# Scores on half the rows, rotary halves exchanged by transfers, two units' values copied at once, another order of block sums: one decoder block on one core

## The chip, the cores and the metric

The kernel runs on one core of one Trainium2 chip. The metric is the device time of one execution in microseconds. A core has TensorE (PE in the profile; its loads of weights are PEld), VectorE (DVE), ScalarE (ACT), GpSimd (POOL) and SyncE (SP), each with a queue of its own that it works off in order. SP issues the transfers (DMA) of this kernel. Matrix products land in PSUM, which has eight banks of 128 x 512 f32; everything else is in SBUF.

## What is computed

One decoder block over 512 tokens of width 1024: a SwiGLU feed-forward layer, a token-mixing layer, a second SwiGLU layer, each behind an RMS norm with shift, scale and gate from a conditioning vector, and a final RMS norm. The change lies in the mixing layer and, in one place, at the start of the second feed-forward layer. Cut to what matters:

```python
def apply_rope(t, cos, sin):
    t1, t2 = jnp.split(t, 2, axis=-1)
    return jnp.concatenate([t1 * cos - t2 * sin, t2 * cos + t1 * sin], axis=-1)

# token_mixing: proj = u @ w_in, split into p, q, k, v, gate_logits
q = apply_rope(q.reshape(B, S, N_ATTN_HEADS, HEAD_DIM), cos, sin)   # 12 heads of 64
k = apply_rope(k.reshape(B, S, N_ATTN_HEADS, HEAD_DIM), cos, sin)
for gi, (window, dilation) in enumerate(((128, 1), (512, 4), (2048, 16))):
    # 4 heads each: query t attends to keys t - j*dilation, j = 0..window // dilation
    o, lse = dilated_window_attention(...)
# groups are combined by the softmax of their log denominators
merged = g_pool * (y_pool @ w_pool_branch) + g_attn * (y_attn @ w_attn_branch)
return merged @ w_out
```

## The kernel before

Products with weights keep f32 accuracy by three terms: each weight chunk is split into a high half (`whi`, an ACT copy at L298) and a low half (`wlo`, a DVE subtraction at L310), each activation likewise (`UH`, `UL`), and a product is high x high, high x low and low x high (`mm3`, L341 to L343). Weights come from HBM as chunks of 512 KB into three buffers `raw` (`fetch`, L226); `look` keeps the splits up to three chunks ahead of use, and a chunk is loaded as soon as a buffer is free and the program has reached that call. SP's queue holds these loads in program order.

The order of everything is written out by hand: each engine does its instructions in the order in which the Python emits them. `mm_tile` (L990) is one tile of 128 output features by 512 tokens: 8 k-steps of three 128x512 products; at chosen k-steps it calls hooks, which emit the attention's instructions in between.

The mixing layer runs as follows. `head` makes the first four tiles, q and k of group 0, in four banks `bk`. Before the change each tile held the first or the second 32 features of four heads (`qk_cols`), so that both rotary halves of all heads lay in two banks, row by row. `rope` (L974) made four products with cosine and sine of both banks (L981) and then, for each pair of heads (64 rows), the difference and the sum (L987, L988) into `qt` or `kt`; there a head pair `hp` has 512 columns, and a head's 64 features lie in rows that are spread as two times 32. For groups 1 and 2 the sums also reorder the tokens into four classes, a stride of four elements on the read. Then v of group 0 is made (L1222 to L1225), then eight tiles for q and k of groups 1 and 2, two pool tiles (`pool_diff`, on GpSimd), four class tiles for v of groups 1 and 2 (L1272 to L1278), and the gates.

Attention is worked in units `(kind, n, hp)`: kind 0 is group 0 with a block n of 128 queries, kind 1 is groups 1 and 2 together with a class n of 128 tokens, hp one of two pairs of heads. A unit passes through four steps, spread over three tiles by `hooks` (L1232):

- `at_prep` (L1010): q times a mask that leaves one head's rows (`qz`, L1018), so that a product over all 128 rows gives one head's scores.
- `at_scores` (L1022): the score products (L1035 and L1037 for kind 0, L1041 for kind 1) into the half `h` of one of two banks `bS`, which take turns by unit; then mask and row maximum (L1053), the negated maximum (L1055) and the exponential with its sum (L1058).
- `at_turn` (L1062), a tile later: transposes of the probabilities (L1070) and a copy (L1073 or L1076).
- `at_values` (L1079), another tile later: products with v (L1093) into `bO`, and a copy of it (L1095, for kind 0 after every unit; L1097, for kind 1 after both).

For kind 0 each of eight tiles takes one new unit; for kind 1 each of four tiles takes two.

The second feed-forward layer works pairs of tiles by block sums of activations. `u_steps` (L673) gives the sums (DVE, L679 and L695) and the splits of three of them into high and low halves `S` (ACT at L685, DVE at L686); `ffn2` (L787) emits them as a list `todo` between the first tiles.

Of the kernel before, what the change touches and what calls it, by code (L numbers as in the profile page):

```python
# [8 lines left out]
F32 = mybir.dt.float32  # L9
# [5 lines left out]
P = 128  # L15
# [74 lines left out]

# [46 lines left out]
class Kernel:  # L137
# [535 lines left out]
    def u_steps(self, n):  # L673
# [7 lines left out]
        def split(i, u):  # L681
            def f():
                hi, lo = self.S[i]
                if i < 3:
                    nc.scalar.activation(hi, u, AF.Copy)  # L685
                    v.tensor_tensor(lo, u, hi, op=OP.subtract)  # L686
                    return
                nc.scalar.activation(hi, u.rearrange("p (k t) -> p k t", k=4), AF.Copy)
                v.tensor_tensor(lo, u.rearrange("p (k t) -> p k t", k=4), hi, op=OP.subtract)
            return f  # L690

# [95 lines left out]
    def ffn2(self):  # L787
        self.put, self.now = [], 0
        bk = [self.nb() for _ in range(4)]
        self.head(2, bk, AF.Silu)  # L790
        adds, (s2, s1, s0, last) = self.u_steps(2)
        self.todo = adds[:3] + [s0, adds[3], s2, adds[4], s1, adds[5]]
        do = lambda n: [self.todo.pop(0)() for _ in range(n)]
        for j in range(2):
            self.ffn_post(j, self.ffn_silu(j, bk[2 * j]), bk[2 * j + 1])
            do(2 + j)
# [4 lines left out]
        self.ffn(2, 4, last)  # L801

# [170 lines left out]

    def rope(self, pa, pb, dst, classes=1):  # L974

        v = self.nc.vector
        t = [self.rt.tile([P, 528], F32, name=f"rt{i}")[:, :T] for i in range(4)]
        for o, x, y in ((t[0], pa, self.cos), (t[1], pb, self.sin), (t[2], pb, self.cos), (t[3], pa, self.sin)):  # L980
            v.tensor_tensor(o, x, y, op=OP.mult)  # L981
        for half in (0, 1):
            rows = slice(64 * half, 64 * half + 64)
            cols = slice(T * half, T * half + T)
            src = [x[rows].rearrange("p (i c) -> p c i", c=classes) for x in t]
            to = [dst[r, cols].rearrange("p (c i) -> p c i", c=classes) for r in (slice(0, 64), slice(64, 128))]
            v.tensor_tensor(to[0], src[0], src[1], op=OP.subtract)  # L987
            v.tensor_tensor(to[1], src[2], src[3], op=OP.add)  # L988

# [19 lines left out]

    def at_prep(self, u):  # L1010

        kind, n, hp = u
        gs, toks = self.at_tokens(u)
        qz = self.aw.tile([P, T], F32, name="qz")
        for i, g in enumerate(gs):
            q = self.qt[g][:, hp * T:hp * T + T]
            for h in range(2):
                self.nc.vector.tensor_scalar(qz[:, (2 * i + h) * P:(2 * i + h + 1) * P], q[:, toks],  # L1018
                                             self.hmask[:, h:h + 1], None, op0=OP.mult)
        self.qz[u] = qz  # L1020

    def at_scores(self, u):  # L1022
        kind, n, hp = u
        nc = self.nc
        M = nc.tensor.matmul
        self.si ^= 1
        S = self.bS[self.si]
        qz = self.qz.pop(u)
        gs, toks = self.at_tokens(u)
        for h in range(2):  # L1030
            o = h * 256
            if kind == 0:
                k = self.kt[0][:, hp * T:hp * T + T]
                if n == 0:
                    M(S[:, o + P:o + 2 * P], qz[:, h * P:h * P + P], k[:, 0:P], start=True, stop=True)  # L1035
                else:
                    M(S[:, o:o + 2 * P], qz[:, h * P:h * P + P], k[:, (n - 1) * P:(n + 1) * P], start=True, stop=True)  # L1037
            else:
                for i, g in enumerate(gs):
                    k = self.kt[g][:, hp * T:hp * T + T]  # L1040
                    M(S[:, o + i * P:o + i * P + P], qz[:, (2 * i + h) * P:(2 * i + h + 1) * P], k[:, toks],  # L1041
                      start=True, stop=True)
        p = self.aw.tile([P, T], F32, name="prob")
# [7 lines left out]
        for h in range(2):  # L1051
            cs = slice(h * 256 + c0, h * 256 + 256)
            nc.vector.tensor_tensor_reduce(p[:, cs], S[:, cs], mask[:, c0:], 1.0, 3.0 * NEG, op0=OP.add, op1=OP.max,  # L1053
                                           accum_out=mx[:, h:h + 1])
# [24 lines left out]
    def at_values(self, u):  # L1079
# [4 lines left out]
        for h in range(2):  # L1084
# [7 lines left out]
            for i, (blk, v) in enumerate(srcs):  # L1092
                M(o, pt[:, blk * P:blk * P + P], v, start=i == 0, stop=i == len(srcs) - 1)  # L1093
        if kind == 0:
# [78 lines left out]
    def mix(self):  # L1173
        nc, tc = self.nc, self.tc
        v, M = nc.vector, nc.tensor.matmul
        self.prob, self.probT, self.pd, self.qz = {}, {}, {}, {}
        self.si = self.ti = 0
        outer = ExitStack()
# [3 lines left out]
        with tc.tile_pool(name="ma", bufs=1) as ma, tc.tile_pool(name="rt", bufs=1) as self.rt, \  # L1182
# [29 lines left out]
            for n in range(4):  # L1212
                if n:
                    self.split(self.pos + n - 1)
                    self.fetch()
                if n == 3:
                    self.at_prep((0, 0, 0))
# [13 lines left out]

            def hooks(new, extra=(), nxt=()):  # L1232
                h = {}
# [3 lines left out]
                for i, u in enumerate(sc):  # L1237
                    h.setdefault(3 + i, []).append(lambda u=u: self.at_turn(u))
                for i, u in enumerate(new):
                    if u not in self.qz:  # L1240
                        h.setdefault(i, []).insert(0, lambda u=u: self.at_prep(u))
                    h.setdefault(5 + i, []).append(lambda u=u: self.at_scores(u))
                for u in nxt:
                    h.setdefault(6 + len(new) - 1, []).append(lambda u=u: self.at_prep(u))
                for k, f in extra:
# [13 lines left out]
            b = self.mm_tile(hooks([], nxt=g23[0]))  # L1259
            self.pool_diff(0, b)  # L1260
            b = self.mm_tile(hooks(g23[0], nxt=g23[1]))
            self.pool_diff(1, b)
# [85 lines left out]
    def build(self):  # L1348
# [23 lines left out]
        self.ones = tl("ones", P)  # L1372
        self.invf, self.hmask, self.icnt, self.ident = cst[:, 0:1], cst[:, 1:3], cst[:, 3:35], cst[:, 35:163]
        self.cst = cst
# [143 lines left out]
def constants():  # L1518
    i = np.arange(P)
    invf = (ROPE_THETA ** (-np.arange(0, HEAD_DIM, 2) / HEAD_DIM)).astype(np.float32)  # L1520
    hm = np.stack([(i % 64 // 32 == h) for h in range(2)], axis=1).astype(np.float32)
    cnt = np.zeros((P, 32), np.float32)
    for t in range(2):
        for half in range(2):
# [4 lines left out]
    q, k = i[:, None], i[None, :]  # L1529
    return np.concatenate([invf[i % 32][:, None], hm, cnt, np.eye(P, dtype=np.float32),  # L1530
                           neg(k >= q), neg(k <= q), neg((k <= q) & ((q - k) % 4 == 0))], axis=1)
# [42 lines left out]
```

## Time and profile before

Three runs took 1013.68, 1013.88 and 1016.19 us; the median is 1013.88.

| what | us |
|---|---|
| the profiled execution's own time | 1014.89 |
| its span, first to last instruction | 1013.1 |
| granted clock of TensorE, mean | 0.999 |
| DVE, v1 to the last class tile (378 to 516), low halves L310 | 23.0 |
| the same, masks L1018 | 15.3 |
| the same, rotary products L981 | 15.3 |
| the same, rotary sums L987 and L988 | 4 x 5.7 |
| ACT busy, 378 to 535 | 54.7 |
| DVE busy, 378 to 535 | 105.5 |
| TensorE busy, 378 to 535 | 156.7 |

The profile is of one execution. A busy time is the union of an engine's instructions. TensorE's matmuls overlap, one starting before the last has run out, and their ends are modelled; so for TensorE the distance between starts tells its pace better than the length of a record. An f32 matmul leaves two records of load and product, the split products of `mm3` one each. The chain of waits is followed back from the last instruction, and its pieces do not overlap.

### The profile page before, as it was taken

The page shows a single profiled execution, that of the slowest core. Times are in us where ns is not written, and L with a number is a line of the kernel's source. Part 1 is how long each engine was busy: PE and PEld are TensorE (multiplying, and loading weights), DVE is VectorE, ACT ScalarE, POOL GpSimd, SP SyncE. Part 2 cuts the span into 40 slices and gives each one's busy share as a digit, 9 for nine tenths or more (in the row PEclk, how much of TensorE's full clock was granted, in tenths as well). Part 3 has the DMA queues.
Part 4 walks back from the last instruction along what each step waited for, and adds up shares of the span by engine and source line. Part 5 has one row for each costly group of instructions (what it writes and reads, how often), then busy time and mean ns, then how long its engine had stood idle before and what let it go on. Part 6 is the DMA issues. An engine that isn't in the chain of part 4 may idle for free.

```text
span 1013.1 us, 15788 instructions
## 1 busy us (share of the span) xinstructions
PE 1004.4 (99%) x6460; PEld 912.8 (90%) x6460; DVE 763.9 (75%) x1117; ACT 442.8 (44%) x674; POOL 26.9 (3%) x31
## 2 busy tenths in 40 slices
PE   9999999999999999999999999999999999999997
PEld 7888999989899999889988888998899899998997
DVE  7989979789797677878447776577787776676754
ACT  6443644525435443334424323454365255352553
POOL 0000000000000000008000000000000000000002
PEclk9999999999999999999999999999999999999999
DMA  9755456455454323122155773412344234241312
GB/s 338 274 202 209 146 160 221 149 173 169 152 182 136 104 77 104 61 65 84 32 199 177 257 270 107 125 56 69 88 167 125 81 105 146 84 137 51 100 47 83
DMA packets 43146, 139.61 MB, mean 138 GB/s; under 512 B 4929, under 2 KB 8257, under 8 KB 43074
## 3 DMA queue, kind: packets, MB, share of 16 engines
q1 hardware_dynamic: 42498, 138.08, 41.4%
q8 instruction: 50, 0.82, 0.3%
q10 hardware_dynamic: 576, 0.52, 0.2%
q14 instruction: 22, 0.18, 0.0%
HBM read 135.82 MB, written 2.77 MB: 137 GB/s over the span
## 4 chain that ended last, share of the span: by engine, by line
PE 87%; DVE 7%; issue 2%; DMA 2%; ACT 1%; POOL 0%; SPq 0%; POOLq 0%; DVEq 0%; ACTq 0%
PE bank L342 15%; PE bank L343 15%; PE bank L341 15%; PE bank L719 10%; PE bank L721 10%; PE bank L720 10%; DVE wlo L310 2%; PE bank L1501 1%; PE bank L1503 1%; PE bank L1505 1%; PE bank L1093 1%; PE bank L1272 1%; DVE H L864 1%; PE bank L1273 1%; PE bank L1274 1%
## 5 line engine op out<-in xcount | busy, mean ns | idle before, releaser
L310 DVE TENSOR_TENSOR wlo<-raw,whi 128x1024 fp32r<-128x1024 f32 (+6 forms) x166 | 174.3, 1061 | 66.0 <-ACT whi L298 65.7
L298 ACT ACTIVATE whi<-raw 128x1024 fp32r<-128x1024 f32 (+6 forms) x166 | 149.9, 920 | 49.2 <-DVE raw L242 41.5
L719 PE MATMUL bank<-UH,whi 128*128 128x256 f32 x544 | 150.6, 277 | 0.2 <-ACT u L726 0.2
L721 PE MATMUL bank<-UH,wlo 128*128 128x256 f32 x544 | 150.5, 277 | 0.0
L720 PE MATMUL bank<-UL,whi 128*128 128x256 f32 x544 | 150.5, 277 | 0.0
L341 PE MATMUL bank<-HI,whi 128*128 128x512 f32 (+1 forms) x406 | 146.6, 361 | 0.0
L342 PE MATMUL bank<-HK,whi 128*128 128x512 f32 (+1 forms) x406 | 146.4, 361 | 0.0
L343 PE MATMUL bank<-HI,wlo 128*128 128x512 f32 (+1 forms) x406 | 146.2, 360 | 0.0
L341 PE MATMUL bank<-UH,whi 128*128 128x512 f32 (+1 forms) x400 | 145.9, 365 | 0.0
L343 PE MATMUL bank<-UH,wlo 128*128 128x512 f32 (+1 forms) x400 | 141.8, 355 | 0.5 <-DVE wlo L310 0.5
L342 PE MATMUL bank<-UL,whi 128*128 128x512 f32 (+1 forms) x400 | 141.8, 355 | 0.1
L310 DVE TENSOR_TENSOR wlo<-X,whi 128x1024 fp32r<-128x1024 f32 (+4 forms) x106 | 111.7, 1063 | 33.4 <-ACT whi L298 33.0
L298 ACT ACTIVATE whi<-X 128x1024 fp32r<-128x1024 f32 (+4 forms) x106 | 95.7, 926 | 47.8 <-DVE X L242 47.0
L719 PE MATMUL bank<-SH,whi 128*128 128x256 f32 x408 | 113.8, 279 | 0.1
L720 PE MATMUL bank<-SL,whi 128*128 128x256 f32 x408 | 113.6, 278 | 0.0
L721 PE MATMUL bank<-SH,wlo 128*128 128x256 f32 x408 | 113.6, 278 | 0.0
L719 PEld LDWEIGHTS bank<-UH,whi 128*128 128x128 f32 x544 | 102.1, 188 | 0.7 <-ACT u L726 0.4
L720 PEld LDWEIGHTS bank<-UL,whi 128*128 128x128 f32 x544 | 102.4, 188 | 0.3
L721 PEld LDWEIGHTS bank<-UH,wlo 128*128 128x128 f32 x544 | 102.1, 188 | 0.0
L342 PEld LDWEIGHTS bank<-HK,whi 128*128 128x128 f32 x406 | 76.3, 188 | 11.8 <-DVE HK L647 0.4
L341 PEld LDWEIGHTS bank<-HI,whi 128*128 128x128 f32 x406 | 76.5, 188 | 11.5
L343 PEld LDWEIGHTS bank<-HI,wlo 128*128 128x128 f32 x406 | 76.4, 188 | 11.6
(227 smaller groups left out, 1761.1 us busy)
## 6 DMA issues: line engine op xcount, KB each, us to landing
ada<-wada SPq DMA_DIRECT2D x47, 512.0 KB, 5.2
raw<-wmix SPq DMA_DIRECT2D x44, 512.0 KB, 3.7
raw<-wf1i SPq DMA_DIRECT2D x32, 512.0 KB, 4.3
raw<-wf2i SPq DMA_DIRECT2D x30, 512.0 KB, 3.5
X<-wf2i SPq DMA_DIRECT2D x14, 512.0 KB, 3.5
cs<-wada SPq DMA_DIRECT2D x12, 512.0 KB, 3.5
AR<-wada SPq DMA_DIRECT2D x12, 512.0 KB, 4.3
raw<-wf2o SPq DMA_DIRECT2D x12, 512.0 KB, 3.5
```

What stands on the lines that cost most here:

```text
L298: self.nc.scalar.activation(self.hi[:, y], r[:, x], AF.Copy)
L310: self.nc.vector.tensor_tensor(self.lo[:, y], r[:, x], self.hi[:, y], op=OP.subtract)
L341: M(ps, hi, uh, start=start, stop=False)
L342: M(ps, hi, ul, start=False, stop=False)
L343: M(ps, lo, uh, start=False, stop=stop)
L719: M(o, hi, uh, start=start and p == 0 and k == 0, stop=False, skip_group_check=True)
L720: M(o, hi, ul, start=False, stop=False, skip_group_check=True)
L721: M(o, lo, uh, start=False, stop=k == 3, skip_group_check=True)
L864: v.scalar_tensor_tensor(self.H[m + i], b, gate[:, m + i:m + i + 1], self.H[m + i], op0=OP.mult, op1=OP.add)
L1093: M(o, pt[:, blk * P:blk * P + P], v, start=i == 0, stop=i == len(srcs) - 1)
L1272: M(b, self.UH[k][:, c::4], hi, start=k == 0, stop=False)
L1273: M(b, self.UH[k][:, c::4], lo, start=False, stop=False)
```

## The change

The columns of q and k in a tile are now those of two whole heads (128 in their own order), where they were halves of four heads. A head's 64 features so lie in 64 rows next to each other. Five things follow or go with it:

- The rotary step is in two parts. `rope_a`, after each tile: ACT copies the bank with a sign per row (`self.sign`, +1 for a first half, -1 for a second), four transfers on SP's queue exchange the 32-row halves into another tile, and DVE multiplies the bank with cosine into `qt` or `kt`. `rope_b`, a tile later at k-step 6 (for group 0 during the v products): DVE multiplies the exchanged tile with sine in place and adds it.
- Scores take 64 rows: head h's from rows 64 h to 64 h + 63 of q and k, into bank `bS[h]`, at the half of it that belongs to `hp`. The masks and `at_prep` are gone.
- For kind 0 both units of a block are new in the same tile, every second tile; their scores stand together, and mask, maximum and exponential (`at_exp`) follow for both.
- For kind 0, too, `bO` is copied once after both units.
- In the second feed-forward layer a split's ACT part and DVE part are entries of their own in the list, and the next block sum stands between them.

```diff
-def qk_cols(base, g, second):
-    return np.concatenate([base + (4 * g + h) * 64 + 32 * second + np.arange(32) for h in range(4)])
...
-            for s in (0, 1):
-                ch.append(_fmajor(w_in, qk_cols(base, g, s)))
+            for hp in (0, 1):
+                ch.append(_fmajor(w_in, base + (4 * g + 2 * hp) * 64 + np.arange(P)))
...
+            x = u if i < 3 else u.rearrange("p (k t) -> p k t", k=4)
+            parts = [lambda: nc.scalar.activation(self.S[i][0], x, AF.Copy),
+                     lambda: v.tensor_tensor(self.S[i][1], x, self.S[i][0], op=OP.subtract)]
+            return parts if n else lambda: [f() for f in parts]
...
-        self.todo = adds[:3] + [s0, adds[3], s2, adds[4], s1, adds[5]]
+        self.todo = adds[:3] + [s0[0], adds[3], s0[1], s2[0], adds[4], s2[1], s1[0], adds[5], s1[1]]
...
+    def rope_a(self, bank, dst, hp, classes, t, w):
+        nc = self.nc
+        nc.scalar.activation(t, bank, AF.Copy, scale=self.sign)
+        for i in range(4):
+            o = i ^ 1
+            nc.sync.dma_start(w[32 * o:32 * o + 32], t[32 * i:32 * i + 32])
+        by = lambda x: x.rearrange("p (i c) -> p c i", c=classes)
+        nc.vector.tensor_tensor(dst[:, hp * T:hp * T + T].rearrange("p (c i) -> p c i", c=classes), by(bank), by(self.cos),
+                                op=OP.mult)
+
+    def rope_b(self, dst, hp, classes, w):
         v = self.nc.vector
+        d = dst[:, hp * T:hp * T + T].rearrange("p (c i) -> p c i", c=classes)
+        v.tensor_tensor(w, w, self.sin, op=OP.mult)
+        v.tensor_tensor(d, d, w.rearrange("p (i c) -> p c i", c=classes), op=OP.add)
...
-    def at_prep(self, u):
...
+        for i, g in enumerate(gs):
+            for h in range(2):
+                rows = slice(64 * h, 64 * h + 64)
+                q, k = (x[g][rows, hp * T:hp * T + T] for x in (self.qt, self.kt))
+                if kind:
+                    o, ks = slice(i * P, i * P + P), toks
                 else:
+                    o, ks = (slice(0, 2 * P), slice((n - 1) * P, (n + 1) * P)) if n else (slice(P, 2 * P), toks)
+                S = self.bS[h][:, 2 * P * hp:2 * P * hp + 2 * P]
+                nc.tensor.matmul(S[:, o], q[:, toks], k[:, ks], start=True, stop=True, skip_group_check=True)
...
-        if kind == 0:
-            self.nc.vector.tensor_copy(self.o1[:, n, P * hp:P * hp + P], O)
-        elif hp == 1:
-            self.nc.vector.tensor_copy(self.o23[:, n, :256], self.bO[:, :256])
+        if hp == 1:
+            self.nc.vector.tensor_copy(self.o23[:, n, :256] if kind else self.o1[:, n, :], self.bO[:, :256])
...
-            self.rope(bk[0], bk[1], self.qt[0])
-            self.rope(bk[2], bk[3], self.kt[0])
+            to = [(self.qt[0], 0), (self.qt[0], 1), (self.kt[0], 0), (self.kt[0], 1)]
+            sw = [self.qt[2][:, :T], self.qt[2][:, T:], self.kt[2][:, :T], self.kt[2][:, T:]]
+            for i in range(4):
+                self.rope_a(bk[i], *to[i], 1, self.v23[:, i, :], sw[i])
...
+                for i in ((), (0, 1), (2,), (3,))[n]:
+                    self.rope_b(*to[i], 1, sw[i])
...
+                h.setdefault(5, []).extend(lambda f=f, u=u: f(u) for f in (self.at_scores, self.at_exp) for u in new)
...
-            todo = [[(0, n, hp)] for n in range(4) for hp in range(2)]
+            todo = [x for n in range(4) for x in ([(0, n, hp) for hp in range(2)], [])]
+            rest = []
             for g in (1, 2):
                 for dst in (self.qt[g], self.kt[g]):
-                    ps = [self.mm_tile(hooks(todo.pop(0), nxt=todo[0] if todo else ())) for s in range(2)]
-                    self.rope(ps[0], ps[1], dst, 4)
+                    for hp in range(2):
+                        b = self.mm_tile(hooks(todo.pop(0), rest))
+                        rt = [self.rt.tile([P, 528], F32, name=f"rt{2 * i + hp}")[:, :T] for i in range(2)]
+                        self.rope_a(b, dst, hp, 4, *rt)
+                        rest = [(6, lambda dst=dst, hp=hp, w=rt[1]: self.rope_b(dst, hp, 4, w))]
```

More of the change, by code (lines that the diff above doesn't have):

```diff
@@ L800, in ffn2 @@
         self.ffn_pair(3)
-        self.ffn(2, 4, last)
+        self.ffn(2, 4, lambda: [f() for f in last])
     def open_ffn(self):
@@ L1024, in at_scores, with at_exp @@
         nc = self.nc
[L1025 to L1028, printed above, removed]
         gs, toks = self.at_tokens(u)
[L1030 to L1042 removed]
+        for i, g in enumerate(gs):
[4 more added lines that the diff above has]
+                    o, ks = slice(i * P, i * P + P), toks
+                else:
+                    o, ks = (slice(0, 2 * P), slice((n - 1) * P, (n + 1) * P)) if n else (slice(P, 2 * P), toks)
+                S = self.bS[h][:, 2 * P * hp:2 * P * hp + 2 * P]
+                nc.tensor.matmul(S[:, o], q[:, toks], k[:, ks], start=True, stop=True, skip_group_check=True)
+    def at_exp(self, u):
+        kind, n, hp = u
+        nc = self.nc
         p = self.aw.tile([P, T], F32, name="prob")
@@ L1175, in mix @@
         v, M = nc.vector, nc.tensor.matmul
-        self.prob, self.probT, self.pd, self.qz = {}, {}, {}, {}
-        self.si = self.ti = 0
+        self.prob, self.probT, self.pd = {}, {}, {}
+        self.ti = 0
         outer = ExitStack()
@@ L1372, in build @@
         self.ones = tl("ones", P)
[L1373 removed]
+        self.invf, self.sign, self.icnt, self.ident = cst[:, 0:1], cst[:, 1:2], cst[:, 3:35], cst[:, 35:163]
         self.cst = cst
@@ L1520, in constants @@
     invf = (ROPE_THETA ** (-np.arange(0, HEAD_DIM, 2) / HEAD_DIM)).astype(np.float32)
-    hm = np.stack([(i % 64 // 32 == h) for h in range(2)], axis=1).astype(np.float32)
+    sign = np.where(i % 64 < 32, 1, -1).astype(np.float32)
     cnt = np.zeros((P, 32), np.float32)
```

52 lines of the change are left out of this document (8 added, 44 removed).

## The prediction

> **What bounds the kernel now.** I read the page's busy shares first, then its slices, then the start times of TensorE's own instructions, and last the chain of waits inside the mixing stage.
>
> ```profile
> PE 1004.4 (99%) x6460; PEld 912.8 (90%) x6460; DVE 763.9 (75%) x1117; ACT 442.8 (44%) x674; POOL 26.9 (3%) x31
> PEclk9999999999999999999999999999999999999999
> ```
>
> TensorE is occupied for 99% of the span at full clock. A busy share does not tell whether it is at its pace, so I compared starts: 128x512 products follow each other every 0.227 us nearly everywhere (rows at 697.09, 697.31 and 697.54 below). Outside the first 16 us, no place loses over 0.4 us but two, both of which the change touches. Here they are in TensorE's timeline, whose columns are start, length, then the instruction and the idle time before it:
>
> ```profile
> 414.00 0.39 PE L343 MATMUL bank<-UH,wlo 128*128 128x512 f32 x1
> 414.63 0.93 PE L1070 MATMUL bank<-cst,prob 128*128 128x128 f32 x4 [0.24 <-ACT prob L1058]
> ...
> 697.09 0.39 PE L343 MATMUL bank<-UH,wlo 128*128 128x512 f32 x1
> 697.31 0.39 PE L341 MATMUL bank<-UH,whi 128*128 128x512 f32 x1
> 697.54 0.39 PE L342 MATMUL bank<-UL,whi 128*128 128x512 f32 x1
> 698.43 0.50 PE L343 MATMUL bank<-UH,wlo 128*128 128x512 f32 x1 [0.50 <-DVE wlo L310]
> ```
>
> At 414.00 the gap to the next start is 0.63 where 0.23 is the pace, and the four transposes behind it take 0.93 where they need 0.67: 0.62 us lost in all with the second wait inside them (0.40 and 0.22 by the starts). At 697.54 the gap is 0.89: 0.66 lost. So time falls only if TensorE gets less work, or if one of these two waits goes. The work that changes is the scores. The chain of waits, in order of time (start, length, what), gives their price in slots without overlap:
>
> ```profile
> 423.53 0.84 PE bank L1093 x8
> ...
> 425.12 0.86 PE bank L1037 x4
> ...
> 470.96 0.89 PE bank L1041 x8
> ```
>
> One f32 matmul leaves two records. A record of 128x256 scores (L1037) costs 0.86/4 = 0.215 us, one of 128x128 scores (L1041) 0.89/8 = 0.111. The values (L1093) stream only 64 columns and still cost 0.84/8 = 0.105 a record: that floor is not the streaming, and I read it as the load of weights that each record has.
>
> **The change, part by part.**
>
> *Scores with 64 rows.* Before: 8 records of L1035 at 0.111 (0.89), 24 of L1037 at 0.215 (5.16), 64 of L1041 at 0.111 (7.10), together 13.15 us. After, the same 96 records use rows 0-63 and 64-127 in turn and write two different banks, so that the second record of one head can run beside the first of the other. Then 2n records take n+1 slots: a group of 8 takes 5, one of 16 takes 9. The first group saves 3 x 0.111 = 0.33, three groups of 256 columns save 3 x 3 x 0.215 = 1.94, four groups of 16 records save 4 x 7 x 0.111 = 3.11: 5.38 us if loads and matmuls of both halves overlap. If only the matmuls do and loads follow one another at 0.105, the 128-column groups gain nothing (16 x 0.105 = 1.68 against 1.78) and 1.94 stay. If nothing overlaps, 0. No row of this trace has a 64-row matmul; I take 5.38, since the two halves share neither rows nor banks, and keep 0 as the other end.
>
> *The price of going from 128 rows to 64 and back.* Eight groups of scores, 16 changes of shape. Bounds: 0, as between f32 transposes, values and products, where neighbours pay only their slots; and 0.35, when the last matmul must run out (a 128-column record lasts 0.274 at a pace of 0.111, so a tail of 0.163) and the next load (0.19, the PEld row of L1041) is not hidden. A gain below 0 is excluded, nothing is skipped at a change. I take the tail alone, 0.163 x 16 = 2.6 us; the ends are 0 and 5.6.
>
> [...]
>
> *What DVE loses and gets.* Removed: 48 maskings (L1018, 15.3 us), 24 rope products (L981, 15.3), 24 half-tile sums (L987 and L988, 4 x 5.7 = 22.8), 8 copies of O (L1095, 2.3): 55.7. Added: 12 products from the bank, 4 at 0.68 and 8 strided ones at 1.08 (the strided rows of L987), 12 with sine at 0.68, 12 sums, again 4 at 0.68 and 8 at 1.08, 4 copies at 0.42: 2.7 + 8.6 + 8.2 + 2.7 + 8.6 + 1.7 = 32.5. DVE is 23 us lighter, worth nothing in itself as TensorE is the bound, except for one wait: at 404.3 to 412.6 the eight rope instructions and the next low half stand ahead of the reduces (L1053) of a unit scored at 409.3, and that is the wait at 414. In the changed order only one product, one low half, one pair of sine and sum, the next bank's product, a low half and a copy stand ahead of the second pair's reduces, spread over two tiles. -0.62 us. The kept end is 0.
>
> *The next turn after that.* A pair's transposes come six k-steps (4.1 us at 0.69) after its scores for the first unit and seven for the second. One unit needs from 418.29 (reduce) to 420.5 (second sum read) 2.2 us; the second unit follows some 1.2 later on ACT, 3.4 against 4.8. Covered; if DVE were 2 us late with a low half, it would cost 0.1 to 1 us per pair.
>
> *Transfers for the rotary halves.* 12 ACT copies of a bank at 0.60 (L1147's row, same shape), 7.2 us on an engine busy 55 of the 157 us from 378 to 535: hidden. 48 transfers of 64 KB on SP, 0.33 each to issue (a weight issue's row): 15.8 us, and each bank's four are passed by the next weight load. Loads now lead their use by 14 to 18 us (issued at 398.26, read by ACT at 414.97), so 3 us later is hidden. Landing is bounded by the mask load (2.4) and the sine spread (3.9). In the steady tiles the even bank is copied after the exponentials, some 2 us into the odd tile, issued by 3.3, landed by 5.7 to 7.2. DVE waits there with sine's part; behind it stand the next bank's product and a low half needed three tiles ahead, then the next reduces at 11.8. Hidden. At the start 16 transfers go out from 381.4 to 386.6, the last land by 389 to 390.5; four products, three low halves and four sine pairs on DVE, each behind its landing or behind ACT's high half (as now at 386.0, 388.9 and 391.8), end near 394.4 by my count, before the first scores at 396.5. Hidden with 2 us to spare.
>
> *Values of two units copied at once.* Four copies fewer; the bank is next written two tiles later. 0.
>
> *Order of the block sums.* Before, DVE waits 1.19 us for ACT's high half S0, then makes its low half and a sum before the weights' low half: 697.15 + 1.15 = 698.3, against TensorE's need at 697.77. After, the next sum stands where S0's low half stood, and the weights' low half waits only for its own ACT copy: S0's high half ends at 694.84 as now, the chunk's high half at 695.8, its low half by 697.0. -0.66 us. S0's low half moves some 3 us back; its products are four tiles (22 us) away.
>
> **Sum.** -5.4 + 2.6 - 0.6 - 0.7 = -4.1 us. The profiled span of 1013.1 becomes 1009.0, the execution's own 1014.9 becomes 1010.8; the median of the runs shown, 1013.9, lies 1.0 below that execution, and its forecast is 1009.8.
>
> **Rivals.** (B) Loads of the two halves queue behind each other: only the 256-column groups gain. -1.9 + 2.6 - 1.3 = -0.6, 1013.3. For it speaks the floor of 0.105 per record in the values' row; against it, that floor is of full-height loads on one set of rows. (C) The halves run one after the other and only the two waits go: +2.6 - 1.3, 1015.2. (D, slower) The change of shape costs a drained and reloaded array each time, 0.35 at 16 places, with no overlap bought: 5.6 - 1.3 = +4.3, 1018.2. It is slower by over 3 us from 0.27 per change on. For it: the tail of 0.163 and the load of 0.19 are both real rows; against it: PEld fetches the next load at the start of the current matmul everywhere in this trace. (E) Sine's part comes late: landings of 6 to 8 us instead of 4 hold DVE, then the reduces, then a pair's transposes, some 0.75 us for each of four pairs, giving back 3 of the 4.1: 1012.8. Against it: DMA is busy 28% from 393 to 458.
>
> **Chances.** Forecast 0.48, B 0.20, C 0.10, D 0.14, E 0.08. A measurement of this kernel tells 0.3%, 3.0 us, from no change, so the borders are 1010.8 and 1016.9. The forecast's own range, by the price of a change of shape, is 1007.2 to 1012.8; I put 0.44 of its 0.48 below the border (a price up to 0.23 per change) and 0.06 of B, which reaches -3.2 where changes are free: faster 0.50. Slower holds nearly all of D and a little of E: 0.14. The rest, 0.36, is no change. The range for 8 in 10 reaches from 1006.3 to 1016.3, leaving out D and a little at the low end.
>
> **What would show it.** Right: a 16-record group of scores spans about 1.0 us plus a change on each side, the next head's record starting within a few ns of its neighbour; no idle time before L1070's successor near 414 nor before a 512-column product near 697; DVE some 23 us less busy. B shows 128-column groups still at 0.11 a record with 256-column ones halved; C and D show 0.11 and 0.215 and a gap on both sides, of 0.16 or 0.35; E shows DVE idle on a landing of the halves and TensorE idle before transposes. I am wrong if the group's length changes as forecast and the span doesn't.

## The result and the profile after

Six runs of the changed kernel took 1008.48 to 1010.48 us, median 1009.78; six of the kernel before, run beside them, 1013.68 to 1016.19, median 1014.37. The ratio is 0.9951, 95% interval 0.9941 to 0.996: 0.4% to 0.6% faster. The profiled execution took 1009.86 us with a span of 1008.1, against 1014.89 and 1013.1.

The page's busy shares and granted clock after the change:

```profile
PE 999.9 (99%) x6460; PEld 906.7 (90%) x6460; DVE 743.5 (74%) x1053; ACT 450.4 (45%) x686; POOL 26.5 (3%) x31
PEclk9999999999999999999999999999999999999999
```

TensorE is still the bound, with 4.5 us less of busy time. DVE lost 20.4 us and ACT gained 7.6 without the time following either. To see where the 5.0 us of span went, I took the start of TensorE's first instruction in each stage and formed differences:

| stretch, by TensorE's starts | before, us | after, us | difference |
|---|---|---|---|
| start to v1 (code not changed) | 381.57 | 381.99 | +0.42 |
| v1 products | 11.52 | 11.52 | 0 |
| q and k tiles, with the two pool tiles | 73.07 | 70.32 | -2.75 |
| class tiles, to the first product of the pool branch | 46.93 | 45.33 | -1.60 |
| last layer, first 512-column product to first block-sum product | 47.45 | 46.37 | -1.08 |
| other stretches | 452.53 | 452.53 | 0 |

The first row is scatter: the stretch has the same code in all kernels here and took 380.4 to 382.6 us in twelve profiles. The change itself is worth 5.4 us, in three stretches.

The chain of waits of the changed kernel (start, length, what), around the first group of 256-column scores, where L337 to L339 are the products of a q or k tile:

```profile
410.03 0.23 PE bank L339
410.26 1.06 PE bank L1019 x8
411.33 0.43 PE bank L337
411.76 0.24 PE bank L338
...
468.63 1.09 PE bank L1019 x16
469.72 0.55 PE bank L1255
```

Eight records of 256 columns take 1.06 us and sixteen of 128 columns 1.09; before, the same work stood as two groups of 0.86 and two of 0.89. Behind each group the next product takes 0.43 (in the class tiles 0.55) where its pace is 0.23. The records' starts, read one by one, show how the halves run:

```
first group of 256 columns, starts in us:
410.195 410.201   410.514 410.521   410.730 410.737   410.947 410.953   then L337 at 411.259
```

The two heads go in lock step, 6 to 7 ns apart, so that 2n records take n slots of 0.215 us. The first slot lasts 0.32 instead of 0.215: one load is not hidden there. In the trace of loads the group's first load starts at 410.192, 3 ns ahead of its matmul, and the first load of the products behind it at 411.257, 2 ns ahead; between products of one shape a load starts some 0.23 us ahead (before the change, 424.723 for the scores at 424.956).

The cost of a group can be told from its neighbours: the distance between the starts of the product before it and of the second product behind it, less two paces of 0.2275. By that measure all score groups cost 14.08 us before and 10.24 after, 3.84 less.

The two waits that the prediction named are gone. TensorE's timeline (start, length, instruction, and an idle time in brackets where there is one) at the transposes behind the second pair, and at the place in the last layer that corresponds to 697.54 before (11.1 us into its stage, which begins at 686.40 there and at 682.47 here):

```profile
415.29 0.39 PE L339 MATMUL bank<-UH,wlo 128*128 128x512 f32 x1
415.52 0.60 PE L1052 MATMUL bank<-cst,prob 128*128 128x128 f32 x4
415.87 0.48 PE L337 MATMUL bank<-UH,whi 128*128 128x512 f32 x1
```

```profile
693.38 0.39 PE L337 MATMUL bank<-UH,whi 128*128 128x512 f32 x1
693.61 0.39 PE L338 MATMUL bank<-UL,whi 128*128 128x512 f32 x1
693.83 0.39 PE L339 MATMUL bank<-UH,wlo 128*128 128x512 f32 x1
```

Neither has idle time: at 415.52 the next product stands 0.35 us behind the transposes, and at 693.61 the next start comes after 0.22. By the same measure as for the scores the transposes cost 7.58 us instead of 8.32, though one group, at 474.11, is 0.17 us longer than its like.

DVE's groups of the mixing stage after (busy, mean ns | idle time before, and its releaser) show what is left of the rotary step:

```profile
L981 DVE TENSOR_TENSOR rt<-rt,cs 128x512 f32<-128x512 f32 x8 | 5.5, 691 | 6.7 <-DMA rt<-rt 6.7
L1077 DVE COPY o<-bank 128x256 f32<-128x256 f32 x4 | 1.7, 423 | 4.8 <-PE bank L1075 4.8
```

DVE does wait on the transfers, 6.7 us over the eight products with sine. Nothing behind it on DVE was late enough for TensorE to notice.

### The profile page after: what moved, and what is told of

It reads as the page before. It is cut to its first block, busy times and chain, and to the rows that moved or that the text cites. A ratio compares the mean times of both kernels' runs of the same rounds, so it can differ in the third digit from the quotient of the medians.

```text
span 1008.1 us, 15846 instructions
## 1 busy us (share of the span) xinstructions
PE 999.9 (99%) x6460; PEld 906.7 (90%) x6460; DVE 743.5 (74%) x1053; ACT 450.4 (45%) x686; POOL 26.5 (3%) x31
## 4 chain that ended last, share of the span: by engine, by line
PE 94%; DVE 2%; DMA 1%; issue 1%; POOL 0%; ACT 0%; SPq 0%; POOLq 0%; DVEq 0%
PE bank L337 17%; PE bank L338 17%; PE bank L339 17%; PE bank L710 10%; PE bank L712 10%; PE bank L711 10%; PE bank L1484 1%; PE bank L1486 1%; PE bank L1488 1%; PE bank L1075 1%; PE bank L1255 1%; PE bank L1019 1%; PE bank L1256 1%; PE bank L1257 1%; PE bank L1052 1%
## 5 line engine op out<-in xcount | busy, mean ns | idle before, releaser
L306 DVE TENSOR_TENSOR wlo<-raw,whi 128x1024 fp32r<-128x1024 f32 (+6 forms) x166 | 175.5, 1067 | 68.1 <-ACT whi L294 67.8
L337 PE MATMUL bank<-HI,whi 128*128 128x512 f32 (+1 forms) x406 | 146.8, 362 | 0.0
L339 PE MATMUL bank<-HI,wlo 128*128 128x512 f32 (+1 forms) x406 | 146.4, 361 | 0.0
L337 PE MATMUL bank<-UH,whi 128*128 128x512 f32 (+1 forms) x400 | 144.8, 362 | 0.0
L339 PE MATMUL bank<-UH,wlo 128*128 128x512 f32 (+1 forms) x400 | 141.9, 355 | 0.0
L306 DVE TENSOR_TENSOR wlo<-X,whi 128x1024 fp32r<-128x1024 f32 (+4 forms) x106 | 111.6, 1063 | 33.1 <-ACT whi L294 32.7
L339 PEld LDWEIGHTS bank<-HI,wlo 128*128 128x128 f32 x406 | 76.4, 188 | 11.6
L337 PEld LDWEIGHTS bank<-HI,whi 128*128 128x128 f32 x406 | 76.6, 189 | 11.4
```

Of the source, the lines that this page charges most:

```text
L306: self.nc.vector.tensor_tensor(self.lo[:, y], r[:, x], self.hi[:, y], op=OP.subtract)
L337: M(ps, hi, uh, start=start, stop=False)
L339: M(ps, lo, uh, start=False, stop=stop)
```

## The experiments

Ten kernels were run, in three sets, each set on one chip together with runs of the kernel before. Medians of the kernel before were 1015.08, 1014.71 and 1014.62 in them.

### Heads one after the other

All scores of rows 0 to 63 of both units are emitted first, then all of rows 64 to 127:

```diff
-            for h in range(2):
+            for h in hs:
...
-                h.setdefault(5, []).extend(lambda f=f, u=u: f(u) for f in (self.at_scores, self.at_exp) for u in new)
+                h.setdefault(5, []).extend(lambda u=u, j=j: self.at_scores(u, (j,)) for j in range(2) for u in new)
+                h[5].extend(lambda u=u: self.at_exp(u) for u in new)
```

> The changed kernel with the order of the score matmuls altered: all of a pair's scores on rows 0 to 63 first, then all on rows 64 to 127, so that neighbours share their rows. Theory (the gain comes from two halves running at once): a group of 16 records grows from 1.09 to about 1.8 us, one of eight 256-column records from 1.06 to about 1.7, the sum over eight groups by 5 to 6 us, and the time to about 1015.5. Rival (the gain comes from a lighter VectorE and the pairing of units, the overlap is worth nothing): no change, 1009.8.

Measured: 1011.4 us (1010.59 to 1012.37, 6 runs), ratio 0.9966 [0.9954, 0.9977] to the kernel before: part of the loss that was expected, not all. Its chain of waits:

```profile
410.40 1.07 PE bank L1019 x8
...
460.78 1.64 PE bank L1019 x16
```

The 8-record groups did not change (1.07 against 1.06), though four records of one half now stand ahead of the other half's. Only the 16-record groups became longer, 1.64 against 1.09: 13 slots instead of 8. Run in the order of the program, four and four records could share one slot at most and would take 7. So TensorE starts records of the other half ahead of queued ones of the first, taking the order of the program for that of its queue, which no record shows by itself. In the 16-record group the first pair that starts together (460.711 is the group's first start, 461.260 and 461.265 the pair) stands behind four single ones. The pairing is shown to be what saves the time, since losing five slots in each of four groups (20 x 0.111 = 2.2 us) raised the score groups from 10.24 to 12.45. The runs' times show it less clearly: 3.7 us of gain are left of 4.6, and the two intervals overlap. How far ahead TensorE looks, beyond this one case, is not shown.

### One head only

This kernel leaves out the scores of rows 64 to 127, so that half of the attention is not computed:

```diff
-            for h in range(2):
+            for h in range(1):
```

> The changed kernel without the scores of rows 64 to 127: the second head of each pair has no score matmuls, its probabilities come from what its bank held. Theory (two halves run in lockstep, both passes beside each other): a group is as long as with both heads, 1.09 and 1.06 us, the time within 0.5 us of the changed kernel's. Rival (n+1 slots, one half a pass behind the other): each group is one slot shorter, 0.11 or 0.21, in sum 1.2 us.

Measured: 1010.33 us in one run, span 1008.5. Its chain of waits:

```profile
410.75 1.06 PE bank L1019 x4
...
461.08 1.08 PE bank L1019 x8
```

Half the records take the same time (1.06 and 1.08 against 1.06 and 1.09), all groups 10.19 against 10.24. The second head is free; 2n records take n slots and not the n+1 of my forecast.

### Units in two k-steps, first attempt

```diff
-                h.setdefault(5, []).extend(lambda f=f, u=u: f(u) for f in (self.at_scores, self.at_exp) for u in new)
+                for f in (self.at_scores, self.at_exp):
+                    for i, u in enumerate(new):
+                        h.setdefault(5 + i, []).append(lambda f=f, u=u: f(u))
```

> The changed kernel with the scores of a pair's two units at neighbouring k-steps, six products between them: 16 groups, 32 changes between 128 and 64 rows in place of 16, the same matmuls. Theory (each change of shape costs 0.20 us, read from the groups of the changed kernel): 16 more changes, +3.2 us, 1013.0. Rival (the price belongs to the first record of a group and only 0.1 of it to the change): +1.6. Rival (changes are free, the group is long for another reason): 0.

Measured: 1019.93 us (1018.47 to 1020.85), ratio 1.0045 [1.0029, 1.0062]. Too much for any theory of shapes, and the timeline of TensorE tells why:

```profile
474.68 1.56 PE L1019 MATMUL bank<-k,q 64*128 64x128 f32 x8 [1.91 <-DVE q L1035]
476.17 0.81 PE L1257 MATMUL bank<-whi,UH 128*128 128x512 f32 x1
476.78 0.63 PE L1258 MATMUL bank<-wlo,UH 128*128 128x512 f32 x1
```

The second unit's scores were emitted behind the first unit's reduces (L1035), whose banks they share, and waited for them. Two more such waits followed, of 0.79 us at 489.13 and 0.44 at 500.42, and the granted clock was 0.50 from 474.7 to 481.5. The three waits (3.1 us), half of that stretch (3.4, an estimate) and the changes of shape (3.6 by the next run) make up most of the 10.9 us by which the two attention stages are longer. The edit tested a wait and not the price of a change of shape, so I made it again.

### Units in two k-steps, again

Scores of the first unit at k-step 5, of the second at 6, and the exponentials of both behind them at 6:

```diff
-                h.setdefault(5, []).extend(lambda f=f, u=u: f(u) for f in (self.at_scores, self.at_exp) for u in new)
+                for f, late in ((self.at_scores, 0), (self.at_exp, 1)):
+                    for i, u in enumerate(new):
+                        h.setdefault(5 + (late or i), []).append(lambda f=f, u=u: f(u))
```

> The changed kernel, with the second unit's scores one k-step of class products behind the first unit's (k 6 instead of 5), and the exp work of both units behind both, so that no score stands behind a reduce of its own group. Eight more groups of scores, each with two changes of shape more, so 16 more changes and nothing else. Theory (a change of shape costs 0.20 us, the rest is slots): 16 x 0.20 = +3.2 us, a group pair of the short kind 1.72 instead of 1.28, 1013.0 in all. Rival 1 (the saving of pairing comes from the two units standing in one group of 128-row slots, a change costs nothing): 1009.8. Rival 2 (what the earlier run with units apart showed, +10 us, is the price of the changes and not of the reduces): 1020.

Measured: 1012.79 us (1012.48 to 1014.37, 10 runs), ratio 0.9982 [0.9973, 0.9992], 3.0 us above the changed kernel's median. Its chain of waits at the first 256-column pair:

```profile
410.94 0.63 PE bank L1019 x4
411.57 0.43 PE bank L337
412.46 0.63 PE bank L1019 x4
413.09 0.43 PE bank L337
```

Two groups of four now cost 0.84 each, 1.68 together, where one group of eight costs 1.276: 0.40 more for one group, so 0.20 us for a change of shape. That it is the shape and not the group as such, the kernel before shows: a 128-row group between the same products costs 0.876, only 0.016 over its four slots. All score groups cost 13.88 against 10.24: +3.64 for 16 more changes, of which the three class tiles with plain neighbours show 0.27 per change. There a group costs something without any change of shape too: 1.02 per group before, where 8 x 0.111 = 0.89 is the slots.

### Masked scores with the rest of the change

Scores over 128 rows with a masked copy of q, as before, and everything else as after:

```diff
+        qz = self.qz.pop(u)
...
-                rows = slice(64 * h, 64 * h + 64)
-                q, k = (x[g][rows, hp * T:hp * T + T] for x in (self.qt, self.kt))
+                k = self.kt[g][:, hp * T:hp * T + T]
...
-                nc.tensor.matmul(S[:, o], q[:, toks], k[:, ks], start=True, stop=True, skip_group_check=True)
+                nc.tensor.matmul(S[:, o], qz[:, (2 * i + h) * P:(2 * i + h + 1) * P], k[:, ks], start=True, stop=True, skip_group_check=True)
```

> The changed kernel with 128-row scores again, each head's q masked to its 64 rows (48 maskings on VectorE, emitted a tile ahead); the exchange by transfers, the pairing, the single copy and the order of sums stay. Theory: the scores cost 14.1 us again where the 64-row ones cost 10.2, +3.8 us, 1013.6; VectorE 15 us busier, and no wait of TensorE for it. Rival (the lighter VectorE was the gain): more than +3.8, with TensorE idle before scores or transposes. Rival (pairing was the gain): 0.

Measured: 1015.48 us (1014.97 to 1016.48), ratio 1.0004 [0.9995, 1.0014]. Without the 64-row scores nothing of the gain is left. Two waits of TensorE are part of that, which the expectation did not have. The first is my edit's own, since the masks of the first block are emitted late:

```profile
397.36 0.39 PE L339 MATMUL bank<-UH,wlo 128*128 128x512 f32 x1
399.20 1.13 PE L1030 MATMUL bank<-k,qz 128*128 128x128 f32 x8 [1.45 <-issue]
```

The score groups cost 15.32 us; the first of them 2.58 where its eight slots are 0.89, so 1.69 is this wait, and 13.63 against 10.24 remains: 3.4 us for the 64-row scores alone. Standing in one group of two units is worth little without them: 1.74 for a 256-column group here, 1.75 for two groups before. The second wait stands in the class tiles, where the next unit's masks are ahead of DVE's copy of v and TensorE's products wait for that copy, as the timelines of DVE and of TensorE show:

```profile
478.19 2.19 DVE L1011 TENSOR_SCALAR qz<-q,hm 128x128 f32<-128x128 f32 x8
480.30 0.68 DVE L1281 COPY v<-bank 128x512 f32<-128x512 f32 x1
```

```profile
479.70 0.40 PE L1277 MATMUL bank<-whi,UL 128*128 128x512 f32 x1
481.04 0.66 PE L1086 MATMUL bank<-v,probT 128*128 128x64 f32 x4 [0.94 <-DVE v L1281]
```

So in the new order the lighter VectorE is worth up to 0.94 us, beside the 3.4. The wait near 414 stayed away with the masks, so it was not their removal that ended it.

### The block sums' order, both ways

In the changed kernel the list goes back to the old order; in the kernel before, the new order is put in alone:

```diff
-        self.todo = adds[:3] + [s0[0], adds[3], s0[1], s2[0], adds[4], s2[1], s1[0], adds[5], s1[1]]
+        self.todo = adds[:3] + [s0[0], s0[1], adds[3], s2[0], s2[1], adds[4], s1[0], s1[1], adds[5]]
...
-            do((2, 3)[j])
+            do((2, 4)[j])
```

> The changed kernel with the block sums' splits in the old order, the ACT part and the VectorE part of a split side by side. Theory: TensorE waits again for the weights' low half at the start of the third pair of the last layer, 0.66 us by the starts; nothing else moves. Rival (the wait went for another reason): no idle time there.

> The kernel before with the new order of block sums alone. Theory: the wait for the low half near 697.5 is gone, -0.66 us, which a comparison of this kind can hardly tell; the wait near 414 (0.6 us) stays. Rival: another low half or sum is late instead and the wait comes back elsewhere.

With the old order (1009.42 us in one run) TensorE's timeline has the wait again:

```profile
692.06 0.39 PE L338 MATMUL bank<-UL,whi 128*128 128x512 f32 x1
692.95 0.50 PE L339 MATMUL bank<-UH,wlo 128*128 128x512 f32 x1 [0.50 <-DVE wlo L306]
```

The stage from the first 512-column product to the first block-sum product is 47.49 us there against 46.37, +1.12; that the whole run is not slower is the unchanged first stretch, 1.5 us shorter in this profile. With the new order alone in the kernel before the same stage is 46.37 instead of 47.45, 1013.44 us in all (1012.88 to 1014.77, 10 runs), ratio 0.9988 [0.9979, 0.9998]. Its wait near 414 stays, as it should:

```profile
413.29 0.39 PE L343 MATMUL bank<-UH,wlo 128*128 128x512 f32 x1
413.88 0.93 PE L1065 MATMUL bank<-cst,prob 128*128 128x128 f32 x4 [0.21 <-ACT prob L1053]
```

So this part stands on its own and is worth 1.1 us by TensorE's starts; the difference of the medians, 1.3, lies within the scatter of the first stretch.

### Sine's part at once

`rope_b` directly behind `rope_a`, for the first block and for each tile:

```diff
-                        rest = [(6, lambda dst=dst, hp=hp, w=rt[1]: self.rope_b(dst, hp, 4, w))]
+                        self.rope_b(dst, hp, 4, rt[1])
```

> The changed kernel with sine's part emitted right behind the transfers, not a step later: VectorE stands at each landing, ahead of the next tile's low half. Theory (TensorE has slack of several us behind VectorE): VectorE idles some 2 to 4 us at each of 12 landings, TensorE loses 0 to 1 us. Rival (the later step is what keeps the transfers off the path): reduces and low halves come late, +4 us or more.

Measured: 1013.84 us (1012.13 to 1016.12, 10 runs), ratio 0.9991 [0.9981, 1.0]. DVE's timeline shows it waiting for each landing, and TensorE's what that does:

```profile
387.48 0.69 DVE L981 TENSOR_TENSOR q<-q,cs 128x512 f32<-128x512 f32 x1 [1.05 <-DMA q<-v]
390.07 0.69 DVE L981 TENSOR_TENSOR k<-k,cs 128x512 f32<-128x512 f32 x1 [1.17 <-DMA k<-v]
```

```profile
392.78 0.40 PE L338 MATMUL bank<-UL,whi 128*128 128x512 f32 x1
395.16 0.80 PE L339 MATMUL bank<-UH,wlo 128*128 128x512 f32 x1 [1.98 <-DVE wlo L306]
395.75 0.63 PE L337 MATMUL bank<-UH,whi 128*128 128x512 f32 x1
396.18 0.63 PE L338 MATMUL bank<-UL,whi 128*128 128x512 f32 x1
```

The weights' low half (L306) stands on DVE behind four waits of 1.1 to 1.5 us, and TensorE waits 1.98 for it. Then its products follow each other at 0.43 us instead of 0.227 until 398.6. Stretches of the same kernel (busy time and records of TensorE, granted clock, DMA share, GB/s) confirm that the clock was halved:

```profile
395.20:398.30 3.10, 3.10 (x7) 0.50 0.73 198
398.70:399.80 1.10, 1.10 (x6) 1.00 0.85 290
```

The q and k stage is 75.64 us against 70.32. Of these 5.3 us, 3.8 are lost ahead of the first scores and 1.5 at the transposes of two later blocks, one of which stands idle for 0.56 us at 434.52; there the landings for groups 1 and 2 hold DVE (five waits, 14.5 us in all). And by medians, each against the kernel before beside it, 0.9 us of gain is left of 4.6 (1013.84 against 1014.71). So the later step is a condition of the gain, not a detail of it.

### Twice the transfers

Each exchange in two transfers of 16 rows, 96 in all instead of 48, with the same bytes:

```diff
-            nc.sync.dma_start(w[32 * o:32 * o + 32], t[32 * i:32 * i + 32])
+            for c in (0, 16):
+                nc.sync.dma_start(w[32 * o + c:32 * o + c + 16], t[32 * i + c:32 * i + c + 16])
```

> The changed kernel with each exchange of 32 rows as two of 16: 96 transfers in place of 48, 15.8 us more issuing on SyncE. Theory (transfers are hidden): 0 to +0.5 us in the tiles for groups 1 and 2; at the start 32 transfers take 10.5 us to issue and land near 395, about when the first scores need them at 393 to 396, so up to 2 us there. Rival (SyncE is near its limit): weight loads come late, TensorE idles on them, +3 us or more.

Measured: 1021.02 us in one run, span 1019.3. The timelines of SP's queue and of TensorE:

```profile
381.18 10.04 SPq L974 DMA_DIRECT2D q<-v  x16
391.31 10.94 SPq L974 DMA_DIRECT2D k<-v  x16
```

```profile
399.28 0.80 PE L1020 MATMUL bank<-k,q 64*128 64x128 f32 x4 [2.95 <-issue]
405.57 0.80 PE L1020 MATMUL bank<-k,q 64*128 64x128 f32 x4 [5.49 <-DVE k L983]
```

A transfer of half the bytes takes the queue as long, 10.04/16 = 0.63 us in the first sixteen and 10.94/16 = 0.68 in the next, so it was the number of transfers that counted here. The first 32 take 21 us, and TensorE stands 2.95 and 5.49 us before and inside the first scores, with its clock halved from 399.2 to 409.4. The expectation of at most 2 us there rested on 0.33 us an issue. The later q and k tiles, whose transfers have a tile and more to spare, cost nothing extra: their score groups are 14.97 us apart, as in the changed kernel. The class tiles took 1.1 us more, at a wait of 0.46 for a low half at 481.52; why that half was late is not shown.

### Transfers on two queues

Every second transfer is issued by GpSimd:

```diff
-            nc.sync.dma_start(w[32 * o:32 * o + 32], t[32 * i:32 * i + 32])
+            (nc.sync, nc.gpsimd)[i % 2].dma_start(w[32 * o:32 * o + 32], t[32 * i:32 * i + 32])
```

> The changed kernel, with every second exchange transfer of the rotary halves issued on GpSimd's queue instead of SyncE's. Theory (the first 16 transfers have 1.5 us of slack, steady ones more; none is on the chain that ends last): the last of the first 16 lands up to 4 us earlier if the issue price of 0.63 us belongs to the queue, VectorE's sine products end earlier, TensorE's starts do not move, 1009.8 within 0.3%. Rival (landing time rather than issue order sets it, or GpSimd issues more slowly than SyncE): the last lands no earlier or later than 393.4; with over 1.5 us later TensorE waits ahead of the first scores and the time is 1011 or more. If it is faster by over 0.3% a wait that the profile did not name is on the chain.

Measured: 1008.6 us (1008.48 to 1009.21, 4 runs), ratio 0.994 [0.9925, 0.9955]. SP's, GpSimd's and DVE's timelines:

```profile
383.04 2.47 SPq L973 DMA_DIRECT2D k<-v  x4
```

```profile
382.93 1.96 POOL L973 DMA_DIRECT2D k<-v  x4
```

```profile
392.44 0.69 DVE L981 TENSOR_TENSOR k<-k,cs 128x512 f32<-128x512 f32 x1
393.15 0.69 DVE L982 TENSOR_TENSOR k<-k,k 128x512 f32<-128x512 f32 x1
```

The last transfer of the first block is issued at 385.5 instead of 391.9. DVE's last sum nevertheless ends 13.3 us behind the start of the v products (at 380.53 here and 381.99 in the changed kernel), as it does in the changed kernel: in neither kernel does a rotary instruction of the first block wait for a landing, and DVE's one wait in that stretch, ahead of a low half, is for ACT's high half, 1.99 us here and 2.03 there. With both queues at work the landings of the first block came 2.1 to 2.9 us behind their issue, median 2.5, where it was 1.9 to 2.0, median 2.0. Every stretch of the table above is within 0.1 us of the changed kernel's but the first, unchanged one (380.53 against 381.99). The interval overlaps the changed kernel's, so no gain is shown.

## Why the prediction was right, point by point

The forecast of 1009.8 met the median of 1009.78. Not every term under it was as good.

- **What bounds.** TensorE's starts were the right view. DVE's 20 us less, forecast as 23 and worth nothing in itself, shows in no start but at the wait near 414, and there it was not the masks (masked scores). That their removal is worth nothing holds less well in the new order: with the masks back, TensorE waited 0.94 us for DVE in the class tiles.
- **Scores with 64 rows, -5.38 forecast.** The mechanism is shown (heads one after the other; one head only); the term was mis-sized. I gave a group n+1 slots, because I let the second record of one head run beside the first of the other. Both start together, 6 to 7 ns apart in the first 256-column group, so it is n, and half of the 13.15 us of slots goes: -6.57. That loads and matmuls of both halves overlap was an assumption when I wrote it: no row of the kernel before shows it.
- **The price of a change of shape, 0.163 forecast.** Measured 0.20 (0.40 for a further group in the second attempt with the units apart) and 0.22 (0.44, in those groups of the first attempt that show no idle time). That a change costs the tail alone, 0.274 less 0.111, was my estimate, and it left out a load; the starts of the changed kernel's first 256-column group show some 0.1 us of wait and some 0.1 of load that nothing hides, at each side. Eight groups cost 3.2 instead of 2.6. What TensorE does in the wait, no run shows.
- **What I had not counted in the scores:** half the groups fall away, and with them 0.13 us for each of the three that stood between class products, and smaller pieces elsewhere, 0.5 in all. -6.57 + 3.24 - 0.5 = -3.8, against -3.84 measured and -2.8 forecast. Two errors of opposite sign partly cancelled.
- **The wait near 414, -0.62 forecast.** It is gone; the transposes cost 0.73 us less with the 0.17 at 474.11 counted in. The new order of the rotary step and its lighter sums were not tried apart.
- **Block sums, -0.66 forecast, -1.08 measured.** The wait at 697.54 was right. The step that fell short is that I stopped at waits over 0.4 us: behind it, before the change, the starts were late by 0.11 us at 698.43, 0.13 at 713.09 and 0.11 at 713.44, and these went with it.
- **Transfers.** Hidden, as forecast, but at another price. I took 0.33 us an issue from a weight load's row; each took 0.51 to 0.62 and followed the last by 0.55 to 0.67, mostly 0.63, within a bank's four. The sixteen first were issued by 391.9 and not by 386.6, as SP's timeline of the changed kernel shows beside DVE's:

```profile
386.99 4.97 SPq L973 DMA_DIRECT2D k<-v  x8
```

```profile
393.89 0.69 DVE L981 TENSOR_TENSOR k<-k,cs 128x512 f32<-128x512 f32 x1
394.61 0.69 DVE L982 TENSOR_TENSOR k<-k,k 128x512 f32<-128x512 f32 x1
```

  The last landed at 393.4, 0.5 us ahead of the DVE product that reads it. DVE ends at 395.3, and the first scores start at 397.0, 1.7 us later where I had said 2. The cover was there, but thinner than I wrote: twice the transfers broke it.
- **Values of two units copied at once, 0 forecast.** Four copies fell away, the new ones take 0.42 us as counted, and the values' groups cost TensorE 12.91 us against 12.98, measured as for the scores; it was not tried alone.
- **The sum.** -3.84 - 0.73 - 1.08 = -5.65 by groups and -5.43 by stretches, less 0.42 of scatter ahead: -5.0 in the span. By medians the gain is 4.6 us against 4.1 forecast; the forecast still met 1009.78, because the kernel before, measured again beside the changed one, came out 0.5 us above the median that I started from. By stretches the change is worth 5.4 where 4.1 was forecast. That forecast and median agree to 0.02 us is luck.
- **The rivals.** B (loads queue) falls by the 128-column groups, which gained as much as the others in slots, and by the loads of the two halves, which also start 6 to 7 ns apart. C (no overlap) falls by one head only. D (0.35 for a change) falls by the 0.20; that a change drains the array, as D has it, no run shows. E (sine's part late) showed its first sign, DVE idle on the halves for 6.7 us, without its second, waits ahead of the transposes, beyond the 0.17; sine's part at once shows what it would have been, with 0.56 us idle ahead of transposes.

## What to carry to other kernels

Here two f32 matmuls of 64 rows, on different halves of the rows and writing different banks, cost as much as one when they stood next to each other in the program (a group took 1.09 us with both heads and 1.08 with one; one bank for both was not tried); the price was 0.20 us for each change between 128 and 64 rows, 0.27 in the class tiles, so gather them into as few groups as the banks allow. When a partition exchange goes from VectorE to transfers, count the transfers first (one of 16 rows held SP's queue for 0.63 to 0.68 us, one of 32 mostly for 0.63), and put the instruction that reads them a step later, behind work that is needed sooner: read at once, they left 0.9 of the 4.6 us. A busy share of 99% is no measure of a chance: of the 5.4 us gained here, 1.8 were waits and delays of under a microsecond, found by the distances between starts.

## What the hardware showed that was not expected

- TensorE overtakes, though each engine is said above to work its queue off in order: a record for the other half of the rows started ahead of records of the first that the program emits earlier. Four records of one half ahead of four of the other cost nothing (1.07 against 1.06 us); eight ahead of eight lost five of eight slots (1.64 against 1.09).
- In three runs a pause of TensorE cost twice. With an idle time of 1.98 us (sine's part at once) the granted clock was 0.50 for 3.4 us from the pause's end, which added about 1.6 us. With one of 1.91 (units in two k-steps, first attempt) it was 0.50 for 6.8 us, which by half of the stretch is an estimate of 3.4. With 2.95 and 5.49 one after the other (twice the transfers) it was 0.50 for 10.2 us, the second pause included. After 1.45 us (masked scores) it stayed at 1.00. The means of the four executions are 0.997, 0.996, 0.994 and 0.999, against 0.999 in the changed kernel. The three stretches are close to one, two and three times the first; what sets their length, no run shows.
- A transfer of 32 rows between two on-chip tiles held SP's queue for 0.55 to 0.67 us, mostly 0.63, and one of 16 rows for 0.63 to 0.68 by the mean of sixteen, against 0.33 for a weight load of eight times the bytes in the prediction's row. In the changed kernel a weight load right behind such transfers held the queue for 0.52 to 0.53, where most others there still took 0.33. GpSimd issued the same transfers at 0.50. With one queue, landing came 1.9 to 2.1 us behind the issue.
